# Fewer filling products on TensorE, and pair 0's receptance product cut in two around the norms' product

## The chip, the cores and the metric

The kernel runs on one core of one Trainium2 chip. The metric is the device time of one execution in microseconds (us), given as the median of several runs. Beside the timed runs there is one profiled execution, whose trace is read here; its span goes from its first to its last instruction.

## The reference, cut to what matters

Two post-norm layers over 512 tokens of 1024 channels in float32. Each layer is a SwiGLU feed-forward half step, a token mixer, and a second feed-forward half step, with a layer norm after each. The mixer of the first layer is a neighbourhood attention, that of the second a bidirectional RWKV-7 time mixing. What the change touches lies in the second mixer:

```python
xr, xw, xk, xv, xa, xg = (x + xx * mix[i] for i in range(6))
r = xr @ w_rkv[0]
k = xk @ w_rkv[1]
v = xv @ w_rkv[2]
...
kk = (k * k_k).astype(f32).reshape(B, S, H, N)
kk = (kk / jnp.maximum(jnp.linalg.norm(kk, axis=-1, keepdims=True), 1e-12)).reshape(B, S, D)
```

The receptance is `r`. The norm of `kk` is taken for each of the 16 heads. The heads are worked through in 8 pairs of 128 channels; pair 0 is the first 128 channels of `r`.

## The kernel before, in words

The stages follow one another: feed-forward, attention, feed-forward, feed-forward, the projections of the time mixing (`rwkv_project`, lines 580 to 736), its scan (`Scan`, from line 996), a norm, and the last feed-forward. Weights come from device memory through SP's queue and are split into a high and a low part (`split`, L221 on ScalarE for the high part, L222 on VectorE or GpSimd for the low part), so that one float32 product is made as three products of the rounded parts (L226, L227, L228). A few products are plain float32; the trace shows each of these as two records on TensorE.

**Who sets the order.** The tile layer plans the program: it simulates the engines and puts each engine's instructions in the order in which they come ready there, the earlier in the program first. Inside `manual_schedule(engines=...)` the engines that are named keep the order of the program. In `rwkv_project` that is TensorE alone, from L661 on; VectorE, ScalarE, GpSimd and SP's queue are planned there. In `Scan` it is TensorE, ScalarE and VectorE; GpSimd and SP's queue are planned. In the first stage nothing is by hand. `behind(...)` puts instructions behind a named one in the same engine's order without waiting for it. An instruction waits at the head of its engine's queue until its operands are there, and everything behind it waits too.

**Filling products.** `busy(out, n)` (L324 to L326) issues n products of the identity with itself into a bank of PSUM that nobody reads. They stand at seven places: 11 ahead of the first transposes (`k.fill = {0: 11}`, L1619, used in `to_channels` at L331), 8 in attention (L973), 11 and 12 just ahead of the projections (L499, L663), 33 when the scan starts (L1105), 17 ahead of the scan's slot -2 (L1190), and twice 9 behind the scan (L749, L754).

**The piece of the projections that is cut.** After the key projection has filled eight banks, TensorE runs, in this order: `rank(0)` and `rank(1)` (L612, 8 plain float32 products each), the norms' product (`ss`, L692: 8 products of 128x512 with a 16-column weight, one for each bank's squares, which ScalarE makes at L676), and pair 0's receptance product (`pr`, L700: 8 products with the weight `wr`). The eight inputs of `pr` are the mixes of `raws(0, dram["xr"])` (L648 on VectorE), each also stored to device memory by SP (L649). They live in the tile `tmp`, which has four buffers; the eight mixes of `raws(3, dram["xv"])` use the same four just before them, and a buffer comes free when its store has landed and its product is done. When `ss` is ready VectorE clamps it (L695) and takes reciprocals (L696), and SP stores the result (L697), which the scan reads at L1209. VectorE also makes the mixes of the gate's low rank at L617 here. Then the halves of the decay input are split (L703, by way of L221 and L222, behind the last mix in VectorE's order), and the decay products start (`decays(0)`, L715 by way of L226 to L228).

**The start of the scan.** SP loads the constants and pair 0's operands (L1102, L1207 to L1211, L1229, L1231); TensorE runs the front of pair 0 (L1234, then L226 to L228), VectorE and ScalarE work on it (L1237 to L1271), the Gram products follow (L1293, masked on VectorE at L1298, copied by SP at L1305), and then the receptance products of the other pairs (L1001, called from L1079), whose inputs SP loads at L1057 and whose weights it loads at L1062.

Of the kernel before, what the change touches and what calls it, by code (L numbers as in the profile page):

```python
# [23 lines left out]
ND = D // P  # L24
# [74 lines left out]
class Trunk:  # L99
# [480 lines left out]
    def rwkv_project(self, dram, xraw, w_rkv, w1, w2, a1, g1, g2, heads):  # L580

        nc = self.nc
        with self.pool("rwa") as pool:
# [24 lines left out]
            def rank(n, w=None):  # L608
                pp = self.bank()
                w = ranks[:, n] if w is None else w  # L610
                for c in range(ND):
                    nc.tensor.matmul(pp[: w.shape[2]], w[:, c, :], rows[n][c], start=c == 0, stop=c == ND - 1)  # L612
                return pp
# [30 lines left out]
            def raws(i, dst):  # L644

                for c in range(ND):
                    t = self.tmp()
                    self.mixed = nc.vector.scalar_tensor_tensor(t, xx[c], self.col(C_MIX + i, c), xraw[:, c, 1 : S + 1], ALU.mult, ALU.add).ins  # L648
                    nc.sync.dma_start(dst[:, c, :], t)  # L649
                    yield c, t  # L650
# [10 lines left out]
            with self.tc.manual_schedule(engines=MANUAL):  # L661
                acc = [self.bank() for _ in range(ND)]
                self.busy(acc[0], 12)  # L663
                for c in range(ND):
                    with self.behind(*marks):
                        u = k_units[c] if c < LEAD else self.load_rows(w_rkv[1], c * P)
                    for o in range(ND):
                        self.mm3(halves_of(acc[o]), u[:, 0, o * P : (o + 1) * P], u[:, 1, o * P : (o + 1) * P],
                                 *mk.get(c), c == 0, c == ND - 1)
                low_rank(1, a1, 4, ends)  # L670
                with self.behind(ends):
                    list(raws(3, dram["xv"]))
                sqs = [q[:, c, :] for q in (quarters(), quarters()) for c in range(4)]
                for o in range(ND):
                    store(dram["rkv"][1][:, o, :], acc[o])
                    nc.scalar.activation(sqs[o], acc[o], AF.Square, scale=self.col(C_KK, o))  # L676

                pw = rank(0)
                wt = evac()
                nc.scalar.activation(wt, pw, AF.Tanh)  # L680
                evs.append(quarters())
                wts = [evac()[: CH + 1] for _ in range(2)]
                for z in range(2):
                    nc.gpsimd.memset(wts[z][CH:], 1.0)
                    nc.sync.dma_start(wts[z][0:CH], wt[z * CH : (z + 1) * CH])
                low_rank(0, g1[:, :P], 5)
                g1b = pool.tile([P, ND, 32], F32, name="g1b")
                nc.sync.dma_start(g1b, g1[:, P:].rearrange("(c p) f -> p c f", p=P))
                pa = rank(1)
                ss = self.bank()[:HEADS]  # L690
                for o in range(ND):
                    nc.tensor.matmul(ss, heads_t[:, o, :], sqs[o], start=o == 0, stop=o == ND - 1)  # L692
                store(dram["ah"], pa)
                iv = evac()[:HEADS]
                nc.vector.tensor_scalar(iv, ss, 1e-24, None, ALU.max)  # L695
                nc.vector.reciprocal(iv, iv)  # L696
                nc.sync.dma_start(dram["iv"], iv)  # L697
                pr = self.bank()
                for c, t in raws(0, dram["xr"]):
                    nc.tensor.matmul(pr, wr[:, c, :], t, start=c == 0, stop=c == ND - 1)  # L700
                with self.behind(self.lo, self.hi, self.mixed):
                    for z in range(2):
                        self.split(wh[z][: CH + 1, 0, :], wh[z][: CH + 1, 1, :], wts[z])  # L703
                store(dram["rkv"][0][:, 0, :], pr)
                self.spares = None
                more.__exit__(None, None, None)

                def decays(z):
                    u = self.load_unit(w2[z])
                    for t in range(NT):  # L710
                        for h in range(2):
                            pp = self.bank()
                            ws = slice(h * 512, h * 512 + 512)
                            ts = slice(t * P, t * P + P)
                            self.mm3(pp, *(wh[z][: CH + 1, i, ts] for i in range(2)), *(u[: CH + 1, i, ws] for i in range(2)), True, True)  # L715
                            th = evac()
                            nc.scalar.activation(th, pp, AF.Tanh, scale=0.5)
                            nc.vector.tensor_scalar(th, th, -0.5 * DECAY, -0.5 * DECAY, ALU.mult, ALU.add)
                            nc.sync.dma_start(dram["lw"][:, z, t, ws], th)

                decays(0)
                pg = [rank(0), rank(0, g1b)]
                gn = (P, 32)
                for i, n in enumerate(gn):
                    raw = self.tmp()[:n]
                    nc.scalar.activation(raw, pg[i][:n], AF.Tanh, scale=0.5)
                    nc.vector.tensor_scalar(raw, raw, 0.5, 0.5, ALU.mult, ALU.add)
                    self.split(gh[i][:n, 0, :], gh[i][:n, 1, :], raw)
                decays(1)
                ug = [self.load_rows(g2, 0), self.load_unit(g2[P:, :])]  # L730
                for c in range(ND):
                    pp = self.bank()
                    for i, n in enumerate(gn):
                        cs = slice(c * P, c * P + P)
                        self.mm3(pp, ug[i][:n, 0, cs], ug[i][:n, 1, cs], gh[i][:n, 0, :], gh[i][:n, 1, :], i == 0, i == 1)
                    store(dram["g"][:, c, :], pp)
# [259 lines left out]
class Scan:  # L996
# [101 lines left out]
    def run(self, late, lead, ln):  # L1098
        with self.k.tc.manual_schedule(engines=MANUAL_SCAN):
            raw = self.tile("e", [P, S], 2)  # L1100
            for dst, src in ((raw, self.dram["ah"]), (self.tri, self.consts["tri"])):
                self.nc.sync.dma_start(dst, src)  # L1102
            list(self.load(0))
            self.k.split(self.ah[:, 0, :], self.ah[:, 1, :], raw)
            self.k.busy(self.k.bank("c"), 33)  # L1105
            list(self.front(0, 0))
            for n in ("mask", "onesb"):
                self.nc.sync.dma_start(getattr(self, n), self.consts[n])
            self.zs = []
            for _ in range(2):  # L1110
                self.unit()
            self.rs, self.out = self.receptances(), self.outs()
            self.led, self.stored = [], 0
            for n in range(-2, HEADS // 2):
                if n == HEADS // 2 - 1:
                    self.early.tile([P, 56], F32, name="pad")
                    self.opened.close()
                    late.enter_context(self.k.early())
                    self.lw = self.leads(lead, ln)
                self.slot(n)  # L1120
            self.ending = self.finish(HEADS // 2 - 1)
            next(self.ending)
# [59 lines left out]
    def slot(self, n):  # L1182

        threads = {name: getattr(self, f)(m, *a) if self.has(m) else iter(()) for name, f, m, *a in (
            ("f1", "front", n + 2, 1), ("f0", "front", n + 3, 0), ("g0", "grams", n + 2, 0), ("g1", "grams", n + 2, 1),
            ("t0", "tails", n + 2, 0), ("t1", "tails", n + 2, 1), ("v", "values", n + 2), ("b", "bonus", n + 2),
            ("e", "gate", n - 1), ("x", "finish", n - 1), ("n", "turn", n + 1), ("i", "invert", n + 2), ("k", "inverted", n + 1), ("j", "merge", n + 1),
            ("l", "load", n + 3), ("c", "chain", n), ("d", "outputs", n))}
        if n == -2:
            self.k.busy(self.k.bank("c"), 17)  # L1190
        threads["r"], threads["o"] = self.rs, self.out
        threads["w"] = self.lw if n == HEADS // 2 - 1 else iter(())
        for name in SEQ.get(n, SEQ[0]).split():
            next(threads[name], None)
        for name, t in threads.items():
            assert name in "ro" or next(t, 1) == 1, (n, name)
# [403 lines left out]
def trunk_kernel(tc, x, ffn_w_in, ffn_w_out, ln_g, ln_b, cols, w_qkv, b_qkv, bias, mask, w_o, b_o,  # L1600
                 w_rkv, w1, w2, a1, a2, g1, g2, rw_out, heads, tri, smask, onesb, eye, out):
    nc = tc.nc
    with ExitStack() as ctx:
        k = Trunk(ctx, tc)
# [11 lines left out]
        with k.activations(), k.psum(bank=8), k.weights(3):  # L1616
            k.load_x(grid(x))
            xT = k.new_xT()
            k.fill = {0: 11}  # L1619
            for t in range(NT):  # L1620
                k.to_channels(t, k.x[t], xT, (k.bank(), k.bank()))
            list(k.lead(k.ffn_lead(ffn_w_in[0, 0]), xT))
# [93 lines left out]
```

## Time and profile before

| what | value |
|---|---|
| three timed runs | 2238.38, 2242.78, 2242.82 us |
| their median | 2242.78 us |
| the profiled execution's own time | 2241.5 us |
| its span | 2239.7 us |
| mean granted TensorE clock in it | 0.994 |

The profile names engines PE (TensorE's products), PEld (its weight loads), DVE (VectorE), ACT (ScalarE), POOL (GpSimd) and SPq (SP's queue of transfers). A row of the timeline has the start in us from the span's start, the time from the first start to the last end of the instructions in the row, engine, line, operation, what is written and read, and how many instructions are merged in it. In brackets stands how long the engine was idle before it, and what ended that idle time. A row of a stage table has the stretch and its length, then for PE, PEld, DVE, ACT and POOL the busy time and the number of instructions, then the granted TensorE clock, the share of the transfer engines' time and GB/s.

### The profile page before, as it was taken

To read this page: it belongs to the slowest core of one execution; us is meant where nothing else is said; L and a number is where in the kernel's file an instruction comes from. 1 tells how busy PE (TensorE), PEld (TensorE's weight loads), DVE (VectorE), ACT (ScalarE), POOL (GpSimd) and SP (SyncE) were. 2 spreads that over 40 slices of the span, in tenths; PEclk is the share of its full clock that TensorE was granted. 3 is DMA by queue.
4 is the path that set the end of the run, shared out by engine and by line. 5 is a ranking of instruction groups with operands and counts; after the bars stand their busy time and mean duration, and the time that the engine had idled before them with its cause. 6 is when DMAs were issued, how large, how long until landed. Compare 5 with 4: busy or idle time off the path is not lost. (4 is left out here: it accounts for less than half of the span.)

```text
span 2239.7 us, 35440 instructions
## 1 busy us (share of the span) xinstructions
PE 2187.5 (98%) x13972; PEld 1720.2 (77%) x13972; DVE 1063.5 (47%) x1524; ACT 957.6 (43%) x1678; POOL 1409.6 (63%) x1234
## 2 busy tenths in 40 slices
PE   8999999999999999999999999899999999999998
PEld 7888888887888888888888875535666657888886
DVE  2333356376433333643333587325788635333345
ACT  3333345377343333433333433336777633333333
POOL 6878855554487886588787442044776722888754
PEclk9999999999999999999999999999999999999999
DMA  6444463432344445454444545754454743544443
GB/s 199 143 143 147 145 230 97 131 93 84 110 141 144 145 143 170 135 184 141 142 137 140 197 131 191 231 158 126 114 141 111 207 151 99 160 142 136 141 169 122
DMA packets 350498, 328.84 MB, mean 147 GB/s; under 512 B 48458, under 2 KB 277450, under 8 KB 350332
## 3 DMA queue, kind: packets, MB, share of 16 engines
q1 hardware_dynamic: 350332, 326.58, 46.8%
q8 instruction: 110, 1.80, 0.3%
q14 instruction: 56, 0.46, 0.1%
HBM read 262.26 MB, written 47.74 MB: 138 GB/s over the span
## 5 line engine op out<-in xcount | busy, mean ns | idle before, releaser
L222 POOL TENSOR_TENSOR w<-raw,w 128x1024 fp32r<-128x1024 f32 x200 | 489.4, 2449 | 246.3 <-ACT w L221 222.7
L226 PE MATMUL bank<-xT,w 128*128 128x512 f32 x1408 | 549.3, 390 | 0.0
L227 PE MATMUL bank<-xT,w 128*128 128x512 f32 x1408 | 548.0, 389 | 0.0
L228 PE MATMUL bank<-xT,w 128*128 128x512 f32 x1408 | 547.9, 389 | 0.0
L221 ACT ACTIVATE w<-raw 128x1024 fp32r<-128x1024 f32 (+1 forms) x204 | 215.3, 1058 | 329.9 <-POOL ts L780 138.3
L428 DVE SCALAR_TENSOR_TENSOR ar<-bank,tmp 128x512 f32<-128x512 f32 x88 | 60.9, 692 | 578.3 <-PE bank L228 568.7
L228 PEld LDWEIGHTS bank<-xT,w 128*128 128x128 f32 x1408 | 264.3, 188 | 55.3
L227 PEld LDWEIGHTS bank<-xT,w 128*128 128x128 f32 x1408 | 264.4, 188 | 53.7
L226 PEld LDWEIGHTS bank<-xT,w 128*128 128x128 f32 x1408 | 264.4, 188 | 53.5
L809 PE MATMUL bank<-wx,an 128*128 128x512 f32 x792 | 187.3, 389 | 0.0
L1382 POOL TENSOR_TENSOR tm<-qs,zs 128x126 f32<-128x126 f32 (+22 forms) x248 | 106.0, 427 | 124.8 <-DVE qs L1375 74.7
L809 PEld LDWEIGHTS bank<-wx,an 128*128 128x128 f32 x792 | 148.7, 188 | 30.8
L809 PE MATMUL bank<-w,ring 128*128 128x512 f32 x720 | 168.8, 390 | 1.8 <-POOL w L222 1.7
L222 POOL TENSOR_TENSOR wx<-ra,wx 128x512 fp32r<-128x512 f32 x132 | 166.8, 1291 | 3.1 <-ACT wx L221 3.1
L222 DVE TENSOR_TENSOR ring<-ar,ring 128x1024 fp32r<-128x1024 f32 x44 | 131.8, 2996 | 73.3 <-ACT ring L221 73.3
L809 PEld LDWEIGHTS bank<-w,ring 128*128 128x128 f32 x720 | 134.9, 188 | 31.1 <-POOL w L222 2.8
L426 ACT ACTIVATE tmp<-bank 128x512 f32<-128x512 f32 x88 | 52.6, 597 | 223.8 <-PE bank L228 223.7
L222 POOL TENSOR_TENSOR ring<-raw,ring 128x1024 fp32r<-128x1024 f32 x28 | 68.4, 2451 | 96.3 <-ACT ring L221 96.3
L1384 POOL TENSOR_TENSOR zs<-zs,tm 128x126 f32<-128x126 f32 (+22 forms) x248 | 111.8, 451 | 19.4
L221 ACT ACTIVATE wx<-ra 128x512 fp32r<-128x512 f32 x132 | 82.9, 633 | 71.8 <-PE bank L809 67.9
L222 POOL TENSOR_TENSOR w<-late,w 128x1024 fp32r<-128x1024 f32 x30 | 76.0, 2538 | 59.7 <-ACT w L221 59.7
L226 PE MATMUL bank<-xT,ring 128*128 128x256 f32 (+1 forms) x352 | 102.3, 299 | 5.7 <-ACT ring L221 2.9
(275 smaller groups left out, 3777.5 us busy)
## 6 DMA issues: line engine op xcount, KB each, us to landing
raw<-in_ffn_w_in_dram SPq DMA_DIRECT2D x176, 512.0 KB, 3.9
ra<-in_ffn_w_out_dram SPq DMA_DIRECT2D x44, 1024.0 KB, 5.0
late<-d_late SPq DMA_DIRECT2D x34, 512.0 KB, 5.1
late<-in_ffn_w_out_dram SPq DMA_DIRECT2D x28, 512.0 KB, 4.4
raw<-in_w_qkv_dram SPq DMA_DIRECT2D x24, 512.0 KB, 4.1
d_late<-ts SPq DMA_DIRECT2D x44, 256.0 KB, 3.4
d_late<-ra SPq DMA_DIRECT2D x44, 256.0 KB, 2.0
xs<-ar SPq DMA_DIRECT2D x64, 128.0 KB, 2.4
```

The costliest lines, as they stand in the source:

```text
L221: self.hi = self.nc.scalar.activation(h, raw, AF.Copy).ins
L222: self.lo = (eng or self.nc.vector).tensor_tensor(l, raw, h.bitcast(F32), ALU.subtract).ins
L226: nc.tensor.matmul(out, wh, xh, start=start, stop=False)
L227: nc.tensor.matmul(out, wh, xl, start=False, stop=False)
L228: nc.tensor.matmul(out, wl, xh, start=False, stop=stop)
L426: nc.scalar.activation(s, pg, AF.Silu)
L428: nc.vector.scalar_tensor_tensor(raw[:, 3:7:3] if j else raw[:, 0:8:7], halves_of(pu), 0.5, halves_of(s), ALU.mult, ALU.mult)
L809: self.nc.tensor.matmul(acc, lhs, u[:, i], start=bool(first) and m == 0, stop=last and m == 2, skip_group_check=more)
L1382: nc.gpsimd.tensor_tensor(tv, qs[:, s, 0:s].rearrange("p (a o) -> p a o", o=1).broadcast_to([P, s, n]), zs[:, s : s + 1, c0:].broadcast_to ...
L1384: nc.gpsimd.tensor_tensor(zs[:, 0:s, c0:], zs[:, 0:s, c0:], tv, ALU.add)
```

## The change

Three of the seven places lose their filling products: the 11 at the start of the kernel, the 33 and the 17 at the start of the scan. The other four keep theirs. And pair 0's receptance product is cut into two halves of four products: the first four stand ahead of the norms' product in TensorE's order, the last four stay behind it. The bank and the generator of the mixes are set up ahead of both; the same eight mixes, stores and products are made.

```diff
                 pa = rank(1)
+                pr, rs = self.bank(), raws(0, dram["xr"])
+
+                def receptance(n):
+                    for c, t in (next(rs) for _ in range(n)):
+                        nc.tensor.matmul(pr, wr[:, c, :], t, start=c == 0, stop=c == ND - 1)
+
+                receptance(ND // 2)
                 ss = self.bank()[:HEADS]
                 for o in range(ND):
                     nc.tensor.matmul(ss, heads_t[:, o, :], sqs[o], start=o == 0, stop=o == ND - 1)
...
                 nc.sync.dma_start(dram["iv"], iv)
-                pr = self.bank()
-                for c, t in raws(0, dram["xr"]):
-                    nc.tensor.matmul(pr, wr[:, c, :], t, start=c == 0, stop=c == ND - 1)
+                receptance(ND // 2)
...
             self.k.split(self.ah[:, 0, :], self.ah[:, 1, :], raw)
-            self.k.busy(self.k.bank("c"), 33)
             list(self.front(0, 0))
...
-        if n == -2:
-            self.k.busy(self.k.bank("c"), 17)
         threads["r"], threads["o"] = self.rs, self.out
...
             xT = k.new_xT()
-            k.fill = {0: 11}
             for t in range(NT):
```

## The prediction

> **What bounds the kernel now.** I read the page first, then a stage table of the four places that the change touches, then the timeline of one engine at a time there.
>
> ```profile
> span 2239.7 us, 35440 instructions
> ...
> PE 2187.5 (98%) x13972; PEld 1720.2 (77%) x13972; DVE 1063.5 (47%) x1524; ACT 957.6 (43%) x1678; POOL 1409.6 (63%) x1234
> ```
>
> TensorE is busy for 98% of the span, so only its idle gaps and a slower clock can cost time, and a filling product is worth something only where it shortens what stands behind it. The stage table has busy time and count for PE, PEld, DVE, ACT and POOL, then granted clock, transfer share and GB/s:
>
> ```profile
> 15.97:22.80 6.83, 5.71 (x24) 5.39 (x25) 1.29 (x2) 2.49 (x4) 5.66 (x3) 0.50 1.05 374
> 1387.00:1425.70 38.70, 38.70 (x127) 20.83 (x125) 8.89 (x20) 17.06 (x29) 4.41 (x5) 1.00 0.41 158
> 1435.37:1438.10 2.73, 2.73 (x12) 2.44 (x13) 0.46 (x1) 1.08 (x2) 0.00 (x0) 0.60 1.13 351
> 1443.11:1446.10 2.99, 2.95 (x27) 2.34 (x27) 1.37 (x3) 0.71 (x2) 0.00 (x0) 1.00 0.97 301
> 1446.10:1450.38 4.28, 0.01 (x1) 0.01 (x1) 3.33 (x6) 3.93 (x11) 0.00 (x0) 0.91 0.99 324
> 1450.38:1456.39 6.01, 6.01 (x14) 1.71 (x16) 0.84 (x2) 0.00 (x0) 0.00 (x0) 0.50 1.07 309
> ```
>
> The reader is to see three things. From 1387 to 1425.7 TensorE is busy throughout: what the cut product gains or loses ahead of it reaches the scan undiminished. At the scan's start the transfer engines are full (0.97 to 1.13) and TensorE waits for them. And the clock is at half (0.50) in two stretches in spite of the filling products.
>
> **The fills at the start of the kernel.** These are TensorE's rows, and ScalarE's first weight split:
>
> ```profile
> 1.37 4.79 PE L326 MATMUL bank<-ident 128*128 128x128 f32 x22 [1.37 <-POOL ident masks.py:199]
> 13.11 1.09 PE L334 MATMUL bank<-ident,x 128*128 128x128 f32 x8 [1.09 <-DMA x<-in_x_dram]
> 15.97 0.58 PE L226 MATMUL bank<-xT,ring 128*128 128x256 f32 x1 [1.76 <-ACT ring L221]
> 14.86 1.06 ACT L221 ACTIVATE ring<-raw 128x1024 fp32r<-128x1024 f32 x1 [2.15 <-DMA raw<-in_ffn_w_in_dram]
> ```
>
> Eleven fills are 22 records and 4.79 us, over by 6.16. The last transposes start at 13.11 because x lands then, and the first projection at 15.97 because the weight landed at 14.86 and its split ended at 15.92. Nothing waits for the fills: removing them **gains 0**. If the transposes then run at half the clock, the last eight end at 13.11 + 2 x 1.09 = 15.29 instead of 14.20, still ahead of 15.97; and the projection already starts at 0.50. So it **costs 0** too; without that cover it would be at most those 1.09 us.
>
> **The cut product.** VectorE's and TensorE's rows between the ranks and the decays, then one of GpSimd, one of ScalarE, and that of the mixes' stores among the transfers (median 2.1 us from issue to landing):
>
> ```profile
> 1368.23 0.75 DVE L648 SCALAR_TENSOR_TENSOR tmp<-ring,cols,xraw 128x512 f32<-128x512 f32 x1 [0.51 <-DMA d_xv<-tmp]
> 1369.57 0.75 DVE L648 SCALAR_TENSOR_TENSOR tmp<-ring,cols,xraw 128x512 f32<-128x512 f32 x1
> 1370.23 2.84 DVE L617 SCALAR_TENSOR_TENSOR ring<-ring,cols,xraw 128x512 f32<-128x512 f32 x1
> 1373.66 0.74 DVE L648 SCALAR_TENSOR_TENSOR tmp<-ring,cols,xraw 128x512 f32<-128x512 f32 x1
> 1374.98 0.74 DVE L648 SCALAR_TENSOR_TENSOR tmp<-ring,cols,xraw 128x512 f32<-128x512 f32 x1
> 1378.30 0.67 DVE L695 TENSOR_SCALAR ring<-bank 16x512 f32<-16x512 f32 x1
> 1379.00 3.34 DVE L696 RECIPROCAL ring<-ring 16x512 f32<-16x512 f32 x1
> 1382.27 2.63 DVE L648 SCALAR_TENSOR_TENSOR tmp<-ring,cols,xraw 128x512 f32<-128x512 f32 x4
> 1384.83 1.27 DVE L222 TENSOR_TENSOR ring<-ring 65x512 fp32r<-65x512 f32 x2
> ```
>
> ```profile
> 1370.01 7.04 PE L692 MATMUL bank<-ring,heads 128*16 128x512 f32 x16
> 1376.98 3.70 PE L700 MATMUL bank<-tmp,wr 128*128 128x512 f32 x8
> 1382.97 3.70 PE L700 MATMUL bank<-tmp,wr 128*128 128x512 f32 x8 [2.29 <-DVE tmp L648]
> 1386.10 0.80 PE L226 MATMUL bank<-w,ring 65*128 65x512 f32 x1
> ```
>
> ```profile
> 1369.81 2.71 POOL L222 TENSOR_TENSOR w<-raw,w 128x1024 fp32r<-128x1024 f32 x1 [15.27 <-ACT w L221]
> 1382.09 1.15 ACT L221 ACTIVATE ring<-ring 65x512 fp32r<-65x512 f32 x2 [6.27 <-DMA ring<-ring]
> d_xr<-tmp SPq DMA_DIRECT2D x8, 256.0 KB, 2.1
> ```
>
> Before, the norms' product runs at 1370.01, four receptance products at 1376.98, and then TensorE stands for 2.29 us: the other four mixes need the four buffers back, and on VectorE the reciprocal lies in their way until 1382.34. The decays start at 1386.10. The cut takes that stall away, since the four buffers come back before the norms' product is over. But it puts the first four products where their own mixes are late.
>
> Step by step, with VectorE's order kept up to the fourth mix (nothing ahead of it in the program moves). One plain product is two records, and a record takes 6.97 / 16 = 0.436 us (1370.01 to 1376.98), so four products take 3.48 us. The mixes are ready at 1368.98, 1370.32, 1374.40 and 1375.72. Products 0 and 1 run from 1370.01 to 1371.75. Then TensorE waits 2.65 us for the third mix, runs it to 1375.27, waits 0.45 for the fourth, and is through at 1376.59. The norms' product takes 6.97: 1383.56. The last four mixes are done by then: the buffers come back as the first products and stores finish, the third and fourth store landing some 2.1 us after 1374.40 and 1375.72, and four mixes take 2.63. So the last four products run without a stall to 1383.56 + 3.48 = 1387.04. That is **0.94 us later** than 1386.10: a stall of 2.29 goes and two of 3.10 together come.
>
> The unknown here is VectorE's order. If the third and fourth mix go ahead of the L617 that takes 2.84 us while GpSimd's L222 lies over it (its kin take 0.74), the third is still held until 1373.07 and the fourth until 1373.73; then the end is 1385.25, 0.85 earlier. With no wait at all the floor is 1370.01 + 3.48 + 6.97 + 3.48 = 1383.94, a gain of 2.16. The other way, the clamp and the reciprocal now come later, from 1383.56: if they stand ahead of the low halves (L222, 1.27 for two), the first of these ends at 1383.56 + 0.67 + 3.34 + 0.64 = 1388.21, up to 1.17 us after TensorE wants to go on. I take +0.94, between -2.16 and +2.11, because the high halves come at 1382.09 by ScalarE's row, ahead of the norms' end, and the low halves with them. What SP stores from the reciprocal is read only in the scan. The receptance's own store and bank are behind the same end in both kernels. SP's queue takes the last four mixes' stores earlier and the reciprocal's later; nothing on TensorE waits for either before 1425.7.
>
> **The fills at the start of the scan.** TensorE's rows and one of VectorE, then two of SP's queue:
>
> ```profile
> 1425.77 7.63 PE L326 MATMUL c<-ident 128*128 128x128 f32 x66
> 1435.37 1.61 PE L1234 MATMUL a<-tri,lw 128*128 128x128 f32 x8 [1.97 <-DMA lw<-d_lw]
> 1438.05 4.57 PE L326 MATMUL c<-ident 128*128 128x128 f32 x34
> 1443.11 1.16 PE L1293 MATMUL g<-ar,bk 64*128 64x128 f32 x16 [0.48 <-DVE bk L1271]
> 1444.20 1.16 PE L1234 MATMUL a<-tri,lw 128*128 128x128 f32 x8
> 1450.38 6.62 PE L1001 MATMUL y<-az,xs 128*64 128x512 f32 x16 [4.32 <-DMA xs<-in_w_rkv_dram]
> 1458.12 1.29 DVE L1298 TENSOR_TENSOR xs<-g,mask 128x512 f32<-128x512 f32 x2 [6.87 <-PE g L1293]
> ```
>
> ```profile
> 1441.06 2.40 SPq L1057 DMA_DIRECT2D xs<-d_xr  x4
> 1443.51 0.43 SPq L1062 DMA_DIRECT2D xs<-in_w_rkv_dram  x1
> ```
>
> The 66 records of 33 fills end 1.97 us before the front's operand lands, the 34 of 17 fills 0.48 us before VectorE hands over `bk`. Neither delays anything: **gain 0**. What they buy is the clock of 1443.11 to 1446.10 (1.00). Without them I take half. The same eight L1234 take 1.61 in the stretch granted 0.60 and 1.16 at 1.00; by that ratio 2.95 busy us grow by 1.14, by plain doubling by 2.95. Behind them TensorE waits 4.32 us for a weight load (issued at 1443.51, one of a row of loads), and VectorE's chain to the next Gram product has 6.87 us to spare. So it **costs 0**; with the cover gone, 1.14 to 2.95. The receptances at 1450.38 start at half the clock in both kernels; a shift of the start against the clock's steps can shorten or lengthen that stretch of 6.01 us, which I put at -1.5 to +1.5.
>
> [...] The trace adds that 66 fills that ended 1.97 us early left the front at 0.60.
>
> **Sum.** 0 + 0.94 + 0: the profiled execution's 2241.5 becomes 2242.4. The median of the runs shown is 1.28 above that execution, so I forecast 2242.78 + 0.94 = **2243.7**, which is no change within 0.2%, about what a measurement of this kernel can tell from none.
>
> **The rivals.** *Earlier mixes* (0.18): the planner puts the third and fourth mix first, and the cut gains 0.85 to 2.16: 2241.9 to 2240.6. For it: TensorE now asks for these two first. Against it: the planner goes by readiness, and what makes them ready has not moved.
>
> *SP's queue held at the scan's start* (0.18), the slower side. SP is planned, and without 50 fills the plan has the first Gram products earlier against the loads.
>
> ```profile
> 1450.41 0.65 SPq L1305 DMA_DIRECT2D az<-xs  x1
> 1444.30 1.29 DVE L1298 TENSOR_TENSOR xs<-g,mask 128x512 f32<-128x512 f32 x2 [1.25 <-PE g L1293]
> ```
>
> The copy L1305 needs the mask at 1445.59. Put ahead of the weight load at 1443.51 it holds the queue 2.08 us, ahead of the loads at 1441.06 it holds it 4.53, and up to 1.16 more with Gram products at half the clock. It decides as soon as L1305 stands ahead of L1062, for TensorE at 1450.38 waits for just that load: 2243.7 + 4.5 = 2248.2, within 2245.8 and 2249.4. Against it: the transfer engines have a backlog (0.97 to 1.13), which hides part.
>
> *The cold clock counts* (0.12): the weight load lands early enough that the products from 1443.11 are in its place: up to 2243.7 + 2.95 = 2246.7.
>
> **How the numbers follow.** The forecast has 0.52, the rivals 0.18, 0.18 and 0.12. The range goes from 2238.0 (the floor 2240.6, less 1.5 for the clock's steps and about one for the spread of the runs, the lowest of which is 2238.38) to 2250.0 (just over 2249.4). Under 2238.3 is faster by over 0.2%, over 2247.3 slower. Faster gets 0.11: 0.05 of the second case, 0.06 of the first, with an order elsewhere that comes out better. Slower gets 0.25: 0.13 of SP's queue, 0.05 of the clock, 0.07 of the forecast's own width. The rest, 0.64, is within 0.2%.
>
> **What would show it.** Right: L700 in three pieces (two products, one, one) with L648 as the releaser, the norms' product ending about 7 us after them, L226 about 0.9 us later; the first weight product and the L1001 behind the same releasers, the clock at half between 1443 and 1446. Wrong: the third mix ahead of L617; low halves behind the reciprocal; L1305 ahead of L1062 in SP's rows; TensorE's wait for the weight load gone; or another order in a stage that the change does not touch.

## The result, and the profile after

The kernel after takes 2238.04 us in the median of 20 runs (2232.11 to 2243.43), the kernel before in the same comparison 2243.22 (2236.84 to 2246.71). The medians are 5.2 us apart; the ratio, which is taken over all the runs, is 0.9982 with a 95% interval of 0.9973 to 0.9990: 0.18% **faster**, some 4 us, against a forecast of +0.94 us. Two more series (below) gave 0.9994 (0.9985 to 1.0003) for the same kernel and 0.9988 (0.9976 to 1.0000) for it with another order of one queue; the mean of the three is 0.9988, or -2.7 us.

The profiled execution can't carry this by itself: at 2243.43 us it is the slowest of its 20, though the stages that the change touches are faster in it. So I read stages from the profiles and totals from the timed runs. The profile's page of the kernel after, first lines:

```profile
span 2241.6 us, 35197 instructions
...
PE 2178.1 (97%) x13850; PEld 1709.4 (76%) x13850; DVE 1059.6 (47%) x1524; ACT 958.5 (43%) x1678; POOL 1412.8 (63%) x1234
```

TensorE has the 122 records of the 61 filling products less and is 9.4 us less busy; that says nothing yet, since filling products are busy time and no work.

**The scan's start**, TensorE's timeline of the kernel after, to be laid beside the rows from 1425.77 to 1450.38 of before:

```profile
1435.69 2.05 PE L1236 MATMUL a<-tri,lw 128*128 128x128 f32 x8 [9.82 <-DMA lw<-d_lw]
...
1443.87 2.08 PE L1295 MATMUL g<-ar,bk 64*128 64x128 f32 x16 [4.85 <-DVE bk L1273]
1445.88 2.07 PE L1236 MATMUL a<-tri,lw 128*128 128x128 f32 x8
...
1449.16 4.09 PE L1006 MATMUL y<-az,xs 128*64 128x512 f32 x16
1453.18 1.16 PE L1295 MATMUL g<-ar,bk 64*128 64x128 f32 x16
```

The last product ahead of the scan, one of the gate's, starts at 1425.45 in before and at 1425.48 in after, and the Gram product behind the first receptances at 1456.93 and 1453.18: 3.78 us are won in this stretch. The front and Gram products do run slower, as forecast: 2.05 instead of 1.61, 2.08 and 2.07 instead of 1.16 each. But the idle 4.32 us ahead of the receptances are gone (no bracket at 1449.16), and the 16 receptances (records of L1006, in before L1001) take 4.09 us, not 6.62. Of the 3.78 us, 2.53 are won in the receptances. The other 1.25 are won ahead of them: they begin 23.68 us after that gate product instead of 24.93, since the weight load that they need landed earlier (at 1449.12 instead of 1450.33, which is 23.64 us after that product instead of 24.88). Both begin 0.04 us after that landing, also in after, where the small products fill the wait to its end. The stage table of the kernel after (columns as in the prediction; the clock is the third number from the end) has the reason for the faster receptances:

```profile
1426.30:1450.00 23.70, 9.46 (x40) 7.15 (x42) 8.70 (x15) 5.95 (x13) 0.00 (x0) 0.50 0.99 313
1450.20:1453.40 3.20, 3.20 (x19) 0.94 (x17) 2.05 (x3) 2.76 (x8) 0.00 (x0) 1.00 1.05 382
```

In after the clock is at half for 23.7 us, through all the waiting, and goes up at about 1450.1, just when the receptances have begun. In before it was up during the wait and half during the receptances. The same table of before, on the steps of the clock:

```profile
1432.50:1435.90 3.40, 1.44 (x13) 1.24 (x12) 1.12 (x2) 0.65 (x2) 0.00 (x0) 1.00 1.00 335
1435.95:1439.30 3.35, 3.35 (x15) 3.06 (x14) 1.66 (x4) 2.08 (x5) 0.00 (x0) 0.50 1.15 343
1439.40:1442.70 3.30, 3.22 (x29) 3.03 (x28) 2.80 (x5) 0.75 (x1) 0.00 (x0) 1.00 1.04 326
1442.80:1446.10 3.30, 2.95 (x27) 2.35 (x27) 1.62 (x4) 0.71 (x2) 0.00 (x0) 1.00 0.97 302
1446.20:1449.50 3.30, 0.00 (x0) 0.00 (x0) 2.39 (x5) 3.19 (x9) 0.00 (x0) 1.00 0.98 309
1449.65:1453.00 3.35, 2.62 (x8) 0.78 (x10) 1.53 (x3) 0.50 (x2) 0.00 (x0) 0.50 1.05 391
1453.05:1456.40 3.35, 3.35 (x10) 0.89 (x8) 0.00 (x0) 0.00 (x0) 0.00 (x0) 0.50 1.09 243
```

Read the second column (TensorE busy) of a row against the clock of the row below it. After 1.44 busy of 3.40 comes 0.50; after 3.35 comes 1.00; after 0.00 comes 0.50; after 2.62 it stays at 0.50. The fills bought a full clock for 2.95 us of small products, then the wait that these no longer filled lost it for the receptances.

**The cut product**, TensorE's and VectorE's timelines of the kernel after:

```profile
1371.23 1.88 PE L694 MATMUL bank<-tmp,wr 128*128 128x512 f32 x4
1373.64 1.12 PE L694 MATMUL bank<-tmp,wr 128*128 128x512 f32 x2 [0.53 <-DVE tmp L648]
1374.97 1.13 PE L694 MATMUL bank<-tmp,wr 128*128 128x512 f32 x2 [0.20 <-DVE tmp L648]
1376.03 7.04 PE L699 MATMUL bank<-ring,heads 128*16 128x512 f32 x16
1383.00 3.70 PE L694 MATMUL bank<-tmp,wr 128*128 128x512 f32 x8
```

```profile
1372.85 0.74 DVE L648 SCALAR_TENSOR_TENSOR tmp<-ring,cols,xraw 128x512 f32<-128x512 f32 x1
...
1383.30 1.29 DVE L222 TENSOR_TENSOR ring<-ring 65x512 fp32r<-65x512 f32 x2 [2.29 <-ACT ring L221]
1384.51 0.67 DVE L702 TENSOR_SCALAR ring<-bank 16x512 f32<-16x512 f32 x1
1385.21 3.34 DVE L703 RECIPROCAL ring<-ring 16x512 f32<-16x512 f32 x1
```

The three pieces and the releaser are as forecast, the two waits are not: 0.53 and 0.20 us where 2.65 and 0.45 stood in the sum. The third mix starts 1.62 us after the first product behind the ranks does (1372.85 less 1371.23), in before it was 3.65 (1373.66 less 1370.01). From the start of the first product behind the ranks to the decays (1386.13) it takes 14.90 us, against 16.09 before.

**The kernel's start** is later. The first projection begins at 16.22 us instead of 15.97, and the first attention product, behind a TensorE that is busy throughout from about 20 us on, at 54.26 instead of 53.89.

### The profile page after: what moved, and what is told of

Same layout as the page of the kernel before. It is cut to its first block, busy times and chain, and to the rows that moved or that the text cites. A ratio compares the mean times of both kernels' runs of the same rounds, so it can differ in the third digit from the quotient of the medians.

```text
span 2241.6 us, 35197 instructions
## 1 busy us (share of the span) xinstructions
PE 2178.1 (97%) x13850; PEld 1709.4 (76%) x13850; DVE 1059.6 (47%) x1524; ACT 958.5 (43%) x1678; POOL 1412.8 (63%) x1234
```

## The experiments

Theory: the gain is made at the scan's start and by the clock alone. Rivals: the order of SP's queue there, which the planner changed (in after the eighth load of `xv` and two weight loads stand ahead of the copies of `x`, L1307; the opposite of the rival that I had feared); the cut; the start. SP's timeline of before, then of after:

```profile
1450.41 1.36 SPq L1305 DMA_DIRECT2D az<-xs  x2
1452.47 4.63 SPq L1062 DMA_DIRECT2D xs<-in_w_rkv_dram  x3
```

```profile
1449.81 1.56 SPq L1067 DMA_DIRECT2D xs<-in_w_rkv_dram  x2
1451.47 4.34 SPq L1307 DMA_DIRECT2D az<-xs  x2
```

I undid the parts one by one first. "Scan stretch" is the time from the start of the last gate product to the end of the first 16 receptances (start of the Gram product behind them): 31.48 us in before, 27.70 in after. "Rank stage" is from the start of the first product behind the ranks to the start of the first decay product.

**1. The cut alone**, all fills kept.

```diff
...
+                receptance(ND // 2)
                 ss = self.bank()[:HEADS]
...
-                for c, t in raws(0, dram["xr"]):
-                    nc.tensor.matmul(pr, wr[:, c, :], t, start=c == 0, stop=c == ND - 1)
+                receptance(ND // 2)
```

> Before with the cut product alone; all filling products stay. Theory (the gain is made at the start of the scan, by the clock): the stretch from the last gate product to the Gram products of the second direction stays as before, 1425.45 to 1456.93 = 31.5 us, and the whole gains only what the cut gives: 1.2 us if the mixes come as early as in the changed kernel's profile, and a loss of 0.9 if they come as late as in that of before. Rival (the cut makes the gain): the whole is 3 to 4 us faster.

Measured: 1.0025 (1.0016 to 1.0035), slower, the rank stage 14.87 us, the scan stretch 29.23, where the theory had 31.5: the wait ahead of the receptances is there (3.93 us), but the 16 behind it take 5.35 us, not 6.62. The loss is not where the change is. TensorE's and SP's timelines of this kernel, 400 us later:

```profile
1783.73 1.98 PE L1006 MATMUL a<-wv,xv 128*64 128x512 f32 x4 [6.08 <-DMA wv<-in_rw_out_dram]
```

```profile
1773.27 0.91 SPq L1511 DMA_DIRECT2D xs<-in_rw_out_dram  x2
1774.39 0.33 SPq L1500 DMA_DIRECT2D ar<-in_rw_out_dram  x1
1774.82 0.66 SPq L1500 DMA_DIRECT2D wv<-in_rw_out_dram  x1
```

The planner put the load of the first slice of the output weights (`wv`) behind three later slices; in before it is the first of these four. TensorE waits 6.08 us for it. A part tried by itself brought its own order with it, so the total of this kernel says nothing of the cut.

**2. The scan's fills out**, nothing else.

```diff
-            self.k.busy(self.k.bank("c"), 33)
...
-            self.k.busy(self.k.bank("c"), 17)
```

> Before without the 33 and the 17 filling products at the start of the scan; no cut, the first 11 stay. Theory: the products of the front and the Gram products run at half the clock until they meet the receptances, no idle gap of 4.28 us is left ahead of these, the clock rises as they begin, and the stretch of 31.5 us takes 27 to 28.5; the whole is 2.5 to 3.8 us faster. Rival (the cut makes the gain): 31.5 us and no change.

Measured: 0.9985 (0.9975 to 0.9995), the scan stretch 26.77 us. This edit alone gives what the whole change gives. But the order of SP's queue changes with it, as in after.

**3. The start's fills out**, nothing else.

```diff
             xT = k.new_xT()
-            k.fill = {0: 11}
             for t in range(NT):
```

> Before without the 11 filling products at the start of the kernel. Theory: no change within 1 us, the first projection starts at 16 us as before, and the stretch of 31.5 us stays. Rival (the start gives part of the gain, the planner having moved a weight split on ScalarE): up to 2 us faster, seen within the first 30 us.

Measured: 1.0005 (0.9994 to 1.0016), no difference that the runs can tell. The profile has one, though, on TensorE and ScalarE of this kernel:

```profile
13.55 1.67 PE L334 MATMUL bank<-ident,x 128*128 128x128 f32 x8 [0.29 <-DMA x<-in_x_dram]
16.85 0.39 PE L226 MATMUL bank<-xT,ring 128*128 128x256 f32 x1 [1.63 <-ACT ring L221]
```

```profile
14.71 1.15 ACT L221 ACTIVATE xT<-bank 128x512 fp32r<-128x512 f32 x2 [0.81 <-PE bank L334]
15.75 1.05 ACT L221 ACTIVATE ring<-raw 128x1024 fp32r<-128x1024 f32 x1
```

Without the fills the last eight transposes take 1.67 us instead of 1.09, and the planner puts the first weight split behind the evacuation of the last transposes (in before it stands ahead of it, at 14.86). So the split waits for TensorE, and the first projection starts at 16.85, not 15.97. Over all profiles, the first attention product, which starts at 53.89 in before, starts 0.37 to 1.46 us later in the four kernels without these fills (mean 0.97) and -0.48 to 0.96 in the nine others with them (mean 0.30): a loss of about 0.7 us, well inside the interval of the ratio, and with overlapping ranges. (The four are after and experiments 3, 4 and 8.)

**4. The kernel after, once more**, with no edit.

> The changed kernel once more, to see what of its profile comes back. Theory: the stretch of 31.5 us takes 27 to 28.5 again, and the cut's own stretch (the last rank product's end to the first decay product, 16.1 us before) 14.9 to 17.0; the whole 2 to 5 us faster than before. Rival (the earlier clock was the luck of one execution): 30 us or more in that stretch.

Measured: 0.9994 (0.9985 to 1.0003), the rank stage 14.87, the scan stretch 27.46. The stages repeat to a few tenths, the totals do not: see the last section.

**5. The gap filled**: before, with all its fills and 18 more just ahead of the first receptance step. SP's queue keeps the order of before.

```diff
+        filled = n != -2
         for name in SEQ.get(n, SEQ[0]).split():
+            if name == "r" and not filled:
+                self.k.busy(self.k.bank("c"), 18)
+                filled = True
             next(threads[name], None)
```

> The kernel before with all its filling products, and 18 more written just ahead of the first receptance step, into the idle 4.28 us of TensorE that stand there in the profile of before. Clock theory (the gain of the kernel after lies at the scan start: there the products that run at half the clock last until the receptances begin, so that no idle stretch sends the clock down again just then): the receptances begin no more than 0.5 us later than in before, run their 16 products in 3.6 to 4.5 us instead of 6.55, and the stretch from the last gate product to the end of these 16 takes 28 to 29.5 us instead of 31.48; the median falls 1.5 to 3 us, to a ratio of 0.9987 to 0.9993. Rival (the gain comes from the changed order of the queue of SP, in which two weight loads stand ahead of the copies of x, or from a stage elsewhere): the queue of this kernel is that of before, so no gain; the 18 products end late and the ratio is 1.000 to 1.001.

Measured: 0.9976 (0.9967 to 0.9985). TensorE's timeline of this kernel:

```profile
1444.56 4.18 PE L326 MATMUL c<-ident 128*128 128x128 f32 x36
1449.62 3.65 PE L1001 MATMUL y<-az,xs 128*64 128x512 f32 x16 [0.89 <-DMA xs<-in_w_rkv_dram]
1453.21 1.16 PE L1297 MATMUL g<-ar,bk 64*128 64x128 f32 x16
```

The 16 receptances take 3.65 instead of 6.62 us, 2.97 less, though they wait for the same load; the scan stretch is 27.23. (The load landed 1.3 us earlier behind the last gate product than in before, which 18 products that start behind the load's issue do not explain.) Opposite edits, fills out and fills added, do the same thing: they keep TensorE from standing idle just ahead of the receptances. This shows the clock theory with the queue's order unchanged. The total fell by more than expected, though: 0.9976 is 5.4 us, where the scan stretch gives 4.25 in these two profiles and less in the mean of all (below). What gives the rest is open.

**6. The 17 out**, the 33 kept.

```diff
-        if n == -2:
-            self.k.busy(self.k.bank("c"), 17)
         threads["r"], threads["o"] = self.rs, self.out
```

> Before without the 17 filling products of slot -2 alone (the 33 behind the split stay). Clock theory: the 33 end at about 1436, 14 us ahead of the receptances, and the 17 are what raises the clock at about 1447; without them the products behind 1436 run at half the clock up to the receptances as in the kernel after. The stretch of 31.48 us falls to 27 to 28.5 and the ratio is 0.9985 to 0.999, that of the kernel with both sets out (0.9985). Rival (it is the 33, or both): a ratio of 0.9995 to 1.0005.

Measured: 1.0006 (0.9996 to 1.0016), and my division between the two sets was wrong. TensorE's timeline of this kernel:

```profile
1443.64 2.07 PE L1232 MATMUL a<-tri,lw 128*128 128x128 f32 x8
...
1449.84 5.22 PE L1001 MATMUL y<-az,xs 128*64 128x512 f32 x16 [3.14 <-DMA xs<-in_w_rkv_dram]
```

The small products do run slowly (2.07 us for eight records, as in after at 0.50), but the 33 let the first front products run fast (1.16 us for the eight) and early, so the last small products start 2.2 us earlier than in after (1443.64 against 1445.88) and 3.14 us stay idle. What counts is not which set raises the clock but what is left of the wait.

**7. The cut alone, first out slice ahead of the later ones but for one.**

```diff
-            nc.sync.dma_start(w[i], rows(self.w_out, i))
+            ld = nc.sync.dma_start(w[i], rows(self.w_out, i)).ins
+            first = ld if i == 0 else first
...
-                    for c in range(EARLY, ND - 1):
-                        nc.sync.dma_start(w[c], rows(self.w_out, c))
+                    with self.k.behind(first):
+                        for c in range(EARLY, ND - 1):
+                            nc.sync.dma_start(w[c], rows(self.w_out, c))
```

> The cut product alone with all filling products (the kernel that came out at 1.0025), its early out-weight loads held behind the load of the first out-weight slice, as they stand in before. Theory (the cut itself is worth -0.1 to -0.5 us, and the loss came from the two swapped loads 400 us later, a wait of 6.08 us for one slice and the half clock behind it): the wait at 1783 is gone and the ratio is 0.9993 to 1.0003. Rival (the cut itself, or what it moves nearer to it, costs the time): the ratio stays at 1.0015 to 1.0035.

Measured: 1.0012 (1.0002 to 1.0022), between the two. The wait for the first slice fell from 6.08 to 1.31 us; the slice `ar` still stood ahead of it. The rank stage was 14.87.

**8. The kernel after with SP's queue in the order of before** at the scan's start (the loads behind the copies of `x`).

```diff
-            load(hp, one(self.units[i][0]))
+            with self.k.behind(*([self.copied] if hp > 1 else [])):
+                load(hp, one(self.units[i][0]))
...
-                    nc.sync.dma_start(self.xv[:, c, :], self.dram["xv"][:, c, :])
+                    with self.k.behind(*([self.copied] if c == ND - 1 else [])):
+                        nc.sync.dma_start(self.xv[:, c, :], self.dram["xv"][:, c, :])
...
-                load(hp, one(vt)[:, i * D : (i + 1) * D])
+                with self.k.behind(self.copied):
+                    load(hp, one(vt)[:, i * D : (i + 1) * D])
...
-                nc.sync.dma_start(az[own, h], x[own, h, :, 1, :])
+                self.copied = nc.sync.dma_start(az[own, h], x[own, h, :, 1, :]).ins
```

> The kernel after, with the eighth load of xv and the six later loads of receptance weights held behind the two copies of x, as they stand in the queue of SP in before. Clock theory: the order of the queue does nothing to the gain; the stretch from the last gate product to the end of the first 16 receptances stays at 27 to 28.5 us (27.7 in after), and the ratio is that of the two runs of the kernel after, 0.998 to 0.9995. Rival (the order of the queue made the gain): the stretch goes back to 30 to 31.5 us and the ratio to 0.9995 to 1.0005.

Measured: 0.9988 (0.9976 to 1.0000), the scan stretch 26.84. SP's and TensorE's timelines of this kernel:

```profile
1452.26 1.36 SPq L1310 DMA_DIRECT2D az<-xs  x2
1453.68 0.60 SPq L1075 DMA_DIRECT2D xv<-d_xv  x1
1454.97 1.97 SPq L1067 DMA_DIRECT2D xs<-in_w_rkv_dram  x2
```

```profile
1450.89 3.65 PE L1006 MATMUL y<-az,xs 128*64 128x512 f32 x16 [0.27 <-DMA xs<-in_w_rkv_dram]
```

The copies are ahead of the loads again, and the receptances still run in 3.65 us. The queue's order is not what made the gain.

**9. The gap filled on top of experiment 7.** Beside that kernel's edits:

```diff
+        filled = n != -2
         for name in SEQ.get(n, SEQ[0]).split():
+            if name == "r" and not filled:
+                self.k.busy(self.k.bank("c"), 18)
+                filled = True
             next(threads[name], None)
```

> The kernel with the cut product and the held out-weight loads (1.0012) and, on top, the 18 filling products in the gap ahead of the receptances (0.9976 by themselves). Theory A (the cut is worth about -0.8 us: rank end to decay took 14.8 to 14.9 us in five kernels with it and 15.0 to 16.1 in five without): the two add up, 0.997 to 0.998, and the stage from rank end to decay takes 14.7 to 15.0 us. Theory B (the cut costs 1 to 3 us somewhere behind the stage, as the ratios 1.0025 and 1.0012 would have it): 0.9985 to 0.9995.

Measured: 0.9981 (0.9970 to 0.9992), the rank stage 14.87. Its interval covers both theories, so this run by itself settles nothing about the cut.

**10. Uncut, with the reciprocal late**; the later out slices held as in experiment 7.

```diff
-                iv = evac()[:HEADS]
-                nc.vector.tensor_scalar(iv, ss, 1e-24, None, ALU.max)
-                nc.vector.reciprocal(iv, iv)
-                nc.sync.dma_start(dram["iv"], iv)
                 pr = self.bank()
                 for c, t in raws(0, dram["xr"]):
                     nc.tensor.matmul(pr, wr[:, c, :], t, start=c == 0, stop=c == ND - 1)
+                with self.behind(self.mixed):
+                    iv = evac()[:HEADS]
+                    nc.vector.tensor_scalar(iv, ss, 1e-24, None, ALU.max)
+                    nc.vector.reciprocal(iv, iv)
+                    nc.sync.dma_start(dram["iv"], iv)
```

> The kernel before with the product of the norms where it stands and the receptance product uncut, but the clamp, the reciprocal and the store of the norms written behind that product and held behind the last mix (out-weight loads held as in the kernel above). Theory A (what the cut gains is the place of the reciprocal of 3.34 us on VectorE, between the fourth and the fifth mix in before and behind the eighth in the cut kernels): the idle time ahead of the second half of the receptance product falls from 1.2 to 2.3 us to under 0.2, and rank end to decay takes 13.6 to 14.3 us, less than with the cut (14.8), which has two waits of 0.5 and 0.2 us of its own; the ratio is 0.999 to 1.0003. Theory B (the mixes five to eight wait for their buffers, that is for the stores, so the place of the reciprocal hardly matters): an idle time of over 1 us stays, 15 to 16 us, and the ratio is 1.000 to 1.0015.

Measured: 1.0005 (0.9995 to 1.0015). TensorE's timeline of this kernel:

```profile
1370.80 7.04 PE L692 MATMUL bank<-ring,heads 128*16 128x512 f32 x16
1377.77 7.13 PE L696 MATMUL bank<-tmp,wr 128*128 128x512 f32 x16
1384.34 0.80 PE L226 MATMUL bank<-w,ring 65*128 65x512 f32 x1
```

All 8 receptance products (16 records) run without a wait; the rank stage takes 13.54 us, 1.3 less than with the cut. So the stall of 2.29 us in before came of the reciprocal's place on VectorE, ahead of the last four mixes. The cut moved the reciprocal behind them too, and paid 0.7 us in waits of its own; the other 0.6 are in the starts around these waits, which come later than 0.436 us a record would have them. The total does not show the gain: here the slice `ar` stood ahead of `wv` again, and TensorE waits for that:

```profile
1781.23 1.98 PE L1002 MATMUL a<-wv,xv 128*64 128x512 f32 x4 [2.47 <-DMA wv<-in_rw_out_dram]
```

**11. The late reciprocal and the filled gap**, uncut: the edits of experiment 10 and the filling products shown in experiment 9 together. Here `wv` is loaded first.

> The two gains together, without the cut: clamp and reciprocal behind the last mix (rank end to decay 13.6 to 14.3 us instead of 16.1), and 18 filling products in the gap ahead of the receptances. The first out-weight slice is loaded first, as in before. Theory (the two add up, and the kernel with the late reciprocal alone came to 1.0005 only because a later slice was loaded ahead of the first one): -2 us on top of the 0.9976 of the filled gap, 0.9965 to 0.9975, the fastest of all. Rival (what the stage of the norms gives is taken back later whatever the order of the loads): 0.9975 to 0.9985, no better than the filled gap alone.

Measured: 0.9971 (0.9960 to 0.9983), 2235.44 us, the lowest ratio of all: -6.5 us. It is faster than before; after, with 0.9988 in the mean, did not run beside it. The rank stage is 13.54, the scan stretch 27.85. Whether it is faster than the filled gap alone (0.9976) these intervals can't tell.

**12. The cut alone, `wv` loaded ahead of all later slices**, as in before. Against experiment 7:

```diff
-            ld = nc.sync.dma_start(w[i], rows(self.w_out, i)).ins
+            with self.k.behind(*([first] if i == 2 else [])):
+                ld = nc.sync.dma_start(w[i], rows(self.w_out, i)).ins
```

> The cut product alone, all filling products kept, and the first out-weight slice loaded ahead of the third, as in before. Theory (the cut gives 0.2 to 1.3 us in its stage, and the two kernels with it that came to 1.0025 and 1.0012 lost 6.08 and 1.31 us waiting for the first out-weight slice): a wait of under 0.7 us ahead of the first out product and a ratio of 0.999 to 1.0005. Rival (the cut itself costs): 1.001 to 1.0025.

Measured: 0.9986 (0.9974 to 0.9999), no wait ahead of the first out product, the rank stage 14.85, the scan stretch 29.63. The same cut gave 1.0025 with `wv` fourth, 1.0012 with `wv` second, 0.9986 with `wv` first. So the cut itself does not cost, and the 6.08 us of experiment 1 come of the order of four loads. That the order explains the other steps is not shown: 1.31 us are 0.06%, and the step from experiment 12 to 7 is 0.26%, with intervals about 0.1% wide on either side; and in experiments 8, 9 and 11, with `wv` first, TensorE waits 1.47, 1.61 and 1.14 us for it.

Laid side by side, for the 14 profiles. The second column is how long after the last gate product's start the receptances begin, the third the idle time just ahead of them, from the row with its bracket (0 where there is none).

| kernel | receptances begin, us | idle ahead, us | 16 receptances, us | scan stretch, us |
|---|---|---|---|---|
| before | 24.93 | 4.32 | 6.62 | 31.48 |
| cut (1), (7), (12) | 23.95, 24.93, 24.35 | 3.93, 3.62, 4.70 | 5.35, 6.50, 5.35 | 29.23, 31.35, 29.63 |
| start's fills out (3) | 23.79 | 4.37 | 6.14 | 29.86 |
| 17 out (6) | 24.68 | 3.14 | 5.22 | 29.83 |
| late reciprocal (10) | 24.43 | 4.27 | 5.35 | 29.71 |
| after (first run), again (4), queue as before (8) | 23.68, 23.88, 23.26 | 0, 0.38, 0.27 | 4.09, 3.65, 3.65 | 27.70, 27.46, 26.84 |
| scan's fills out (2) | 23.19 | 0.64 | 3.65 | 26.77 |
| gap filled (5), (9), (11) | 23.64, 24.23, 24.27 | 0.89, 0, 0.58 | 3.65 each | 27.23, 27.81, 27.85 |

Seven kernels with 3 us or more idle: a stretch of 30.2 us in the mean, begun at 24.4. Seven with under 1: 27.4, begun at 23.7. The difference is 2.8 us or 0.12%. Of it 2.1 us lie in the receptances, and there the two sets do not overlap: that is the gain by the clock. The other 0.7 come of the weight load, which landed earlier in the second set, with overlapping ranges; no run ties this to the filling products. Before's own stretch is the longest of its seven, so the 3.78 us between the first two profiles overstate the gain.

## Why the prediction was wrong

**The fills at the start of the scan: the step that failed.** I costed them at nothing because "the receptances at 1450.38 start at half the clock in both kernels". In after they start at half the clock too, but it goes up 0.9 us later, where before stays at half for 6; in experiments 2, 4, 5, 8, 9 and 11 all 16 run in 3.65 us. I had the small products' growth right (up to 2.95 us; 0.44 + 0.92 + 0.91 and some for the three products of the split parts) and that the 4.28 us of waiting hide it. I did not carry the step on: what fills the wait also keeps TensorE busy through it, and the clock of the receptances went with that: 0.50 behind 0.00 us busy of 3.30 in before, 1.00 from 1450.1 on behind 3.41 busy of 3.41 in after. I had even quoted the row of 0.01 us busy with the row of 0.50 below it. Measured in place of 0, over seven kernels against seven: -2.1 us in the receptances, and -0.7 ahead of them that no run explains.

The rows of the table above have it: with 3.14 to 4.70 us idle just ahead, the 16 receptances take 5.22 to 6.62 us; with 0 to 0.89, 3.65 to 4.09. It was the kernel before that had the gap, right where it hurt, and experiment 5 filled it.

**The cut product: right in its mechanism, mis-sized.** The 2.29 us stall goes, two waits come, the order on VectorE is as taken up to the fourth mix, and the low halves stand ahead of the clamp (my upper bound of +2.11 did not come). The term that was off is the 2.65 of the first wait, which measured 0.53 (0.49 to 0.53 in seven kernels with the cut). I took the third mix from the profile of before, and there it was late. SP's timeline of before, then of after:

```profile
1363.37 2.37 SPq L649 DMA_DIRECT2D d_xv<-tmp  x1
```

```profile
1364.69 0.38 SPq L649 DMA_DIRECT2D d_xv<-tmp  x1
```

This one issue of a store took SP 2.37 us; the buffer came back late (VectorE waits 2.26 us for `d_xv<-tmp` ahead of a mix) and all mixes behind it were late. In the uncut kernels the stall ahead of the second half was 2.29, 2.17, 1.93, 1.42 and 1.16 us and the rank stage 16.09, 15.97, 15.73, 15.22 and 14.97, 15.6 in the mean; in seven with the cut 14.85 to 14.90. So the cut gives 0.7 us, where I had it cost 0.94. In five more kernels without the cut (experiments 2, 5, 6, 10 and 11) this store or the one next to it took SP 1.2 to 1.6 us, in experiment 3 only 0.4 and 0.5, and in the seven with the cut never over 0.6. So it was no accident of the one profile: the third mix starts 2.78 to 3.65 us behind the first product in six of the seven uncut kernels, 1.49 in experiment 3, and 1.57 to 1.62 in all seven with the cut. Why SP's issues are slow in the uncut kernels and not in the cut ones stays open, and with it why the 2.65 came out as 0.53.

**The start: I wrote that it costs 0 and that without cover it would be at most 1.09.** The cover failed: I had the transposes' own end (15.29) ahead of the projection, but not that a weight split on ScalarE could be put behind their evacuation. About +0.7 us.

**The sum** by these: +0.7 - 0.7 - 2.1 = -2.1 us, or 0.9991, and -2.8 us, or 0.9988, if the earlier landing counts; the three measurements of after have 0.9988 in the mean. Their intervals reach from 0.9973 to 1.0003, so they can't tell the two apart, and the terms at the start and for the cut are smaller than any of them can show.

**The rivals.** *Earlier mixes*, at 0.18, named the right sign for the cut, but by another way than the third mix ahead of L617: L617's place did not change. *SP's queue held* did not come; the planner went the other way, and experiment 8 shows that with the order of before the gain stays. What the copies ahead of the first weight load would have cost, no run shows. *The cold clock counts* did not come: the products from 1443 were hidden, as the forecast had it.

## What to carry to other kernels

Ask of a filling product not whether it ends in time but what TensorE does just ahead of the heavy products (in before 0.00 us busy of 3.30, and 0.50 granted behind it): fill the last wait ahead of them, or leave the small products slow enough to fill it themselves. When one part of a change is tried by itself under a planner, compare each queue's order first; here another order of four loads cost more than the part was worth. And a wait that hangs on a transfer need not carry over to the kernel after: here six of seven kernels without the cut had it, and none with it, so a second profile of before would most likely have shown it again.

## What the runs showed of the hardware that I had not expected

In the profiles of before and after the granted clock is 1.00 or 0.50, and these are all its stretches at 0.50:

| kernel | at 0.50 from, us | for, us | TensorE busy in the 3.41 us just ahead, us |
|---|---|---|---|
| before | 15.97 | 6.83 | 1.09 |
| before | 1435.91 | 3.41 | 1.45 |
| before | 1449.57 | 6.83 | 0.00 |
| before | 1575.86 | 6.83 | 1.36 |
| before | 2234.63 | to the span's end | 0.00 |
| after | 16.48 | 6.83 | 1.41 |
| after | 1426.19 | 23.89 | 3.10 |
| after | 1542.24 | 3.41 | 1.15 |
| after | 1583.20 | 6.83 | 1.80 |
| after | 1627.58 | 6.83 | 0.01 |
| after | 2235.15 | to the span's end | 0.65 |

TensorE stood idle for all of the time ahead, or all but 0.01 us, in only three of the eleven; in six more it was busy for 0.65 to 1.45 us, and once each for 1.80 and 3.10. On the other side, 1.67 to 1.97 us busy of 3.41 had the full clock behind them in before from 5.73, 9.14, 1381.30, 1545.14 and 2183.44 us on, and in after from 2183.95 on. So no one number of busy time parts these two profiles, and the 3.10 is not explained. At half the clock TensorE did half its work: in before's receptances one pair of records follows the other in 0.85 us at 0.50, in those of after in 0.43 at 1.00.

The half clock is one thing that can scatter the runs. Both profiles have a wait for VectorE that ends in the 1540s: 2.66 us up to 1546.85 in before, with 1.00 behind it, and 2.26 us up to 1541.61 in after, with 3.41 us at 0.50 from 1542.24. Twelve runs of one and the same kernel lie up to 13 us apart (2233.62 to 2246.72 in experiment 8), and a gain of 2.8 us needs the mean of many. Time and granted clock go together in part: in the 20 runs of after the slowest has 0.988 and the fastest 0.994, with a correlation of -0.63 over all. How much of the 13 us the clock makes is not shown. In after the half clock from 1627.58 came with a late transfer; TensorE's timeline and the stage table:

```profile
1628.49 1.97 PE L1006 MATMUL a<-xv,wv 128*64 128x512 f32 x4 [4.32 <-DMA wv<-in_w_rkv_dram]
```

```profile
1628.00:1634.30 6.30, 5.81 (x54) 4.20 (x58) 1.94 (x5) 0.28 (x1) 5.28 (x14) 0.50 0.17 55
```

A wait of 4.32 us for one weight, where before has none, and 6.3 us at half the clock (0.50) behind it, in a stage which the change does not touch: some 4 us of waiting and an estimated 3 us of slower products (half of the 5.81 us busy).
